# The tail of a recurrent block one step ahead, its hyperbolic tangent at the end of the block itself

## The chip, the cores and the metric

The kernel runs on one core of one Trainium2 chip. The metric is the device time of one execution, in microseconds; runs are compared by their medians.

## The reference

One layer with a prompt of 2048 tokens and 8 x 8 sample tokens (2112 columns in all) and a width of 1024. From the normalised input `u`, a projection `z = u @ w_in` feeds three branches: a recurrent one (RG-LRU), a dilated attention, and merge gates. The change touches the recurrent branch alone:

```python
xa, new_conv = causal_conv(xa, conv_buf, conv_w, conv_b)       # 4 taps
# rg_lru, in 8 blocks of 128 channels:
gate_a = einsum(x_block, w_a) + b_a ;  gate_x = einsum(x_block, w_x) + b_x
r = sigmoid(gate_a) ;  i = sigmoid(gate_x)
log_a = -8 * r * softplus(-lam)
a = exp(log_a)
u = sqrt(-expm1(2 * log_a)) * (i * x)
h_t = a_t * h_(t-1) + u_t                                      # along the tokens
ya = (hs * silu(ga)) @ w_lru_proj
```

## The kernel before

The order of the instructions is written out by hand: each engine takes its own in the order of the program, and waits only for semaphores. The stages run one after the other: normalising and transposing the input, the attention of the prompt, its gate, **the recurrent branch** (lines 815 to 975), the merge gates with the sample attention spread over them (`gm_block`, from line 991), and the output projections.

In the recurrent branch the loop over `b` does one block of 128 channels at a time. The tokens lie along the free dimension in five chunks `CH` of 512, 512, 384, 384 and 320 columns. A block has two halves of five steps; call them A0 to A4 and B0 to B4.

In A0 to A4, `zT` (24 matmuls, L760) projects one chunk for `xa`, and `evac` copies it (ScalarE, L861) into `xpad`. In between stand the convolutions of the chunks 0 and 1 (`conv`: one ScalarE instruction, L868, then three on VectorE, L870), the first `gates_a`, and the splits of weights into a high and a low half (`w_split`, `split`: a cast on ScalarE, L93, and a subtraction on VectorE, L94).

In B0 to B4, `zT` projects a chunk for the gate `ga`; ScalarE and VectorE make its silu in `sgl` (L964, L965); `gates_b` runs the six gate matmuls of the chunk (L888) on `xh`, the split copy of the convolved chunk that `gates_a` made (cast L879, subtraction L880), and turns them into `rr` and `ii` by sigmoids; then follow `gates_a` of the next chunk and, in B0 to B2, `conv` of the chunks 2 to 4. `xh` has one buffer, the z tiles of `zT` four (two tags of two).

What is left of a block, its tail, is done during the next block. `tail_1` makes `tt` = tanh from `rr` (five instructions, one for each chunk), `tail_2` the exponentials on ScalarE with a square on GpSimd and a product on VectorE, `tail_r` the square roots, and `tail_3` for each chunk a product (L914), the scan (L922), a product with `sgl` on GpSimd (L923) and a store to `Y1` (L924, on SP). Before, tail_1, tail_2 and tail_r stand at A0, A1 and A2, and the five pieces of tail_3 at A2, A3, A4, B0 and B1, each ahead of the convolution that writes the same chunk of `xc`. The tail of block 7 stands in the first `gm_block`. There `states` (its step 4) transposes the last states on TensorE into `hp` (L982).

DMAs are issued on SP in the order of the program: cache copies (`copy`, 480 KB each, one a step), weights (`w_raw`, one buffer), and the stores to `Y1`.

Of the kernel before, what the change touches and what calls it, by code (L numbers as in the profile page):

```python
# [42 lines left out]
def program(tc, I, O, C, upto=99, debug=False):  # L43
# [44 lines left out]
    def ztile(*tags):  # L88
        zi[0] += 1
        return ps.tile([128, 512], F32, name="zt", tag=tags[zi[0] % len(tags)])  # L90

    def split(h, l, src, eng):
        ACT.copy(h, src)  # L93
        eng.tensor_sub(l, src, h.bitcast(F32))  # L94
# [11 lines left out]
    def copy(n=1):  # L106
        for _ in range(n):
            if copies:
                i = dma(*copies.pop())
                if not G.manual:  # L110
                    tc.keep_in_program_order(i)
# [566 lines left out]
    def w_raw(src, nk=8):  # L678
        wr = wzp.tile([128, nk, 128], F32, name="wzr", tag="wzr")
        dma(wr, src)  # L680
        return wr

    def w_split(wr, eng, nk=8):
        w = wzp.tile([128, 2, nk, 128], F32R, name="wz", tag="wz", bufs=2)
        split(w[:, 0], w[:, 1], wr, eng)
        return w

    def wcols(c0):
        return win[:, c0:c0 + 128].rearrange("(k p) c -> p k c", p=128)
# [67 lines left out]
    def zT(z, w, c0, n):  # L757
        for i in range(24):
            k, p = divmod(i, 3)
            PE.matmul(z[:, 0:n], w[:, (0, 1, 0)[p], k, :], (RH, RH, RL)[p][:, k, c0:c0 + n], start=(i == 0), stop=(i == 23))  # L760
# [68 lines left out]
    def par_prep():  # L829
        prt = ps.tile([128, 8, 42], F32, name="prt", tag="tr")  # L830
        for n in range(8):
            PE.transpose(prt[:, n, :], rows[:, n * 128:(n + 1) * 128], ident[0:42, 0:42])
        DVE.tensor_copy(par, prt)
        DVE.tensor_scalar(e_, lam, -1.0, None, ALU.mult)
        DVE.tensor_tensor(e_, e_, lam, ALU.min)
        ACT.activation(e_, e_, AF.Exp)
        DVE.tensor_scalar(y_, e_, 2.0, None, ALU.add)
        DVE.reciprocal(y_, y_)
        DVE.tensor_mul(y_, y_, e_)
        DVE.tensor_mul(q_, y_, y_)  # L840
        DVE.tensor_scalar(c8, q_, 2.0 / 19, 2.0 / 17, ALU.mult, ALU.add)
        for i in (15, 13, 11, 9, 7, 5, 3, 1):
            DVE.tensor_mul(c8, c8, q_)
            DVE.tensor_scalar(c8, c8, 2.0 / i, None, ALU.add)
        DVE.tensor_mul(c8, c8, y_)
        DVE.tensor_scalar(e_, lam, -1.0, 0.0, ALU.mult, ALU.max)
        DVE.tensor_add(c8, c8, e_)
        DVE.tensor_scalar(n8, c8, 8.0, None, ALU.mult)
        DVE.tensor_scalar(c8, c8, -8.0, None, ALU.mult)
# [9 lines left out]
    def evac(c0, n, z):  # L859
        npr = min(n, SEQ - c0)  # L860
        ACT.copy(xpad[:, 3 + c0:3 + c0 + npr], z[:, 0:npr])  # L861
        if npr < n:
            ACT.copy(xsp[:, :, 3:11], z[:, npr:n].rearrange("p (s t) -> p s t", t=8))
# [13 lines left out]
    def gates_a(c0, n):  # L877
        xh = lp.tile([128, 2, 512], F32R, name="xh", tag="xh")
        ACT.copy(xh[:, 0, 0:n], xc[:, c0:c0 + n])  # L879
        DVE.tensor_sub(xh[:, 1, 0:n], xc[:, c0:c0 + n], xh[:, 0, 0:n].bitcast(F32))  # L880
        return xh
# [13 lines left out]
    def tail_1(b):  # L895
        for c0, n in CH:
            ACT.activation(tt[:, c0:c0 + n], rr[:, c0:c0 + n], AF.Tanh, scale=n8[:, b:b + 1])

    def tail_2(b):
        for c0, n in CH:  # L900
            s = slice(c0, c0 + n)
            ACT.activation(rr[:, s], rr[:, s], AF.Exp, scale=c8[:, b:b + 1])
            a2 = lp.tile([128, 512], F32, name="a2", tag="ii", bufs=2)
            POOL.tensor_mul(a2[:, 0:n], rr[:, s], rr[:, s])
            DVE.scalar_tensor_tensor(tt[:, s], a2[:, 0:n], 1.0, tt[:, s], ALU.add, ALU.mult)

    def tail_r(b):
        for c0, n in CH:
            ACT.activation(tt[:, c0:c0 + n], tt[:, c0:c0 + n], AF.Sqrt)

    def tail_3(b, i0=0, i1=5):
        for c0, n in CH[i0:i1]:
            s = slice(c0, c0 + n)
            DVE.tensor_mul(xc[:, s], xc[:, s], tt[:, s])  # L914
            if c0 + n == NT:
                a0 = rr[:, SEQ:NT:8]
                hh = lp.tile([128, 8], F32, name="hh", tag="hh")
                DVE.tensor_mul(hh, a0, par[:, b, 34:42])
                DVE.tensor_add(xc[:, SEQ:NT:8], xc[:, SEQ:NT:8], hh)
                DVE.memset(a0, 0.0)  # L920
            init = 0.0 if c0 == 0 else tt[:, c0 - 1:c0]
            DVE.tensor_tensor_scan(tt[:, s], rr[:, s], xc[:, s], init, ALU.mult, ALU.add)  # L922
            POOL.tensor_mul(sgl[:, s], sgl[:, s], tt[:, s])  # L923
            dma(Y1[b][:, s], sgl[:, s])  # L924
        if i1 < 5:
            return
        POOL.tensor_copy(par[:, b, 4:5], tt[:, SEQ - 1:SEQ])
        POOL.tensor_copy(par[:, b, 34:42], tt[:, SEQ + 7:NT:8])

    for b in range(8):  # L930
        for ci, (c0, n) in enumerate(CH):
            z = early.pop(ci, None) if b == 0 else None
            if z is None:
                z = ztile("z", "S")
                zT(z, wx, c0, n)
            evac(c0, n, z)
            copy()
            if ci == 0:
                gr = lp.tile([128, 2, 128], F32, name="gr", tag="gr")
                dma(gr[:, 0], I["lru_w_a"][0, b])  # L940
                dma(gr[:, 1], I["lru_w_x"][0, b])
                wga = w_split(wgr, DVE)
                wxr = w_raw(wcols((b + 1) * 128 if b < 7 else C_GM))
            if b == 0 and ci == 2:
                par_prep()
            if b and ci < 3:
                (tail_1, tail_2, tail_r)[ci](b - 1)
            if b and ci > 1:
                tail_3(b - 1, ci - 2, ci - 1)
            if ci == 2:  # L950
                POOL.tensor_copy(xsp[:, :, 0:3], par[:, b, 10:34].rearrange("p (s j) -> p s j", j=3))
                gw_ = lp.tile([128, 2, 2, 128], F32R, name="gw_", tag="gw_")
                split(gw_[:, 0], gw_[:, 1], gr, DVE)
                conv(b, *CH[0])
            if ci == 3:
                xh = gates_a(*CH[0])
                conv(b, *CH[1])
        for ci, (c0, n) in enumerate(CH):
            z = ztile("z", "S")
            zT(z, wga, c0, n)  # L960
            if ci == 0:
                wx = w_split(wxr, DVE)
                wgr = w_raw(wcols(1024 + (b + 1) * 128 if b < 7 else C_GM + 128))
            ACT.activation(sgl[:, c0:c0 + n], z[:, 0:n], AF.Sigmoid)  # L964
            DVE.tensor_mul(sgl[:, c0:c0 + n], z[:, 0:n], sgl[:, c0:c0 + n])  # L965
            gates_b(b, c0, n, xh, gw_)
            if ci < 4:
                xh = gates_a(*CH[ci + 1])
            if b and ci < 2:
                tail_3(b - 1, ci + 3, ci + 4)  # L970
            if ci < 3:
                conv(b, *CH[ci + 2])
            copy()
        POOL.tensor_copy(par[:, b, 0:3], xpad[:, SEQ:SEQ + 3])
        POOL.tensor_copy(par[:, b, 10:34].rearrange("p (s j) -> p s j", j=3), xsp[:, :, 8:11])

# [14 lines left out]
    def gm_block(f, w, hooks, gtile):  # L991
        for ci, (c0, n) in enumerate(CH):
            z = ztile("z", "S")
            zT(z, w, c0, n)
            for h in hooks.get(ci, ()):
                h()
            gt = gtile()
            ACT.activation(gt[:, 0:n], z[:, 0:n], AF.Sigmoid, bias=par[:, f % 8, 8 + f // 8:9 + f // 8])  # L998
            dma(Gsc[f][:, c0:c0 + n], gt[:, 0:n])
            copy()  # L1000
            if plan and f:
                for fn in plan.pop(0):
                    fn()

    plan = []
    wm = {0: wx}

    def nextw(f):
        if f + 1 < 16:
            wm[f + 1] = w_split(G.wr, DVE)  # L1010

    def nextr(f):
        if f + 2 < 16:
            G.wr = w_raw(wcols(C_GM + (f + 2) * 128))

    G.wr = wgr
    gm_block(0, wm[0], {0: (lambda: nextw(0), lambda: nextr(0), lambda: tail_1(7), lambda: tail_2(7)), 1: (lambda: tail_r(7), lambda: tail_3(7),), 4: (states,)},
             lambda: lp.tile([128, 512], F32, name="gt0", tag="ii", bufs=2))
    lr.close()
    gts = ExitStack()  # L1020
# [571 lines left out]
```

## Time and profile before

| | |
|---|---|
| median of 3 runs | 2575.45 us (2571.48 to 2576.32) |
| the profiled execution | 2570.03 us, span 2568.3 us |
| TensorE busy | 2501.8 us (97%) |
| VectorE, ScalarE, GpSimd busy | 1541.6, 1082.9, 561.5 us |
| mean granted TensorE clock | 0.992 |

The span is the time from the first to the last instruction of the profiled execution. An engine's busy time leaves out its waits; matmuls overlap, so a busy TensorE is not one at its peak. "Released by" names the instruction whose semaphore ended a wait.

### The profile page before, as it was taken

The numbers are of one execution on the slowest core, as the hardware profiler recorded it, in microseconds if no ns is written. First come the engines' busy times: TensorE is split into PE (matmuls) and PEld (weight loads), VectorE is DVE, ScalarE is ACT, GpSimd is POOL, SyncE is SP. The second block draws the span as 40 slices with busy tenths as digits, with TensorE's granted clock in tenths as the row PEclk, the third lists the DMA queues.
The fourth block names the chain that finished last, engine by engine and source line by source line (L and its number), as shares of the span: only waits on it lengthen the run. The fifth ranks groups of instructions, "written<-read, shape, count | busy, mean of one in ns | idle before, by whom it ended". The sixth has DMA issues, their size and how long they took to land. (4 is left out here: it accounts for less than half of the span.)

```text
span 2568.3 us, 44715 instructions
## 1 busy us (share of the span) xinstructions
PE 2501.8 (97%) x15196; PEld 2341.9 (91%) x15196; DVE 1541.6 (60%) x4805; ACT 1082.9 (42%) x3327; POOL 561.5 (22%) x897
## 2 busy tenths in 40 slices
PE   8999999999999999999999999999888999999999
PEld 7999999999999999999988888888878899998988
DVE  6744686777786776647665667737765723432322
ACT  5534453443553443444455655535466511211110
POOL 4423322221221221213233334320001012200000
PEclk9999999999999999999999999999999999999999
DMA  5443564555453433337633333345555479633332
GB/s 146 114 132 101 144 178 142 160 158 152 144 166 100 122 115 111 89 98 235 214 112 131 130 112 123 130 161 176 182 171 184 150 213 339 197 112 119 115 121 66
DMA packets 311288, 376.73 MB, mean 147 GB/s; under 512 B 54914, under 2 KB 254926, under 8 KB 308220
## 3 DMA queue, kind: packets, MB, share of 16 engines
q1 hardware_dynamic: 297028, 356.31, 45.2%
q0 software_dynamic: 14032, 17.57, 2.5%
q8 instruction: 120, 1.97, 0.3%
q14 instruction: 108, 0.88, 0.1%
HBM read 293.55 MB, written 168.31 MB: 180 GB/s over the span
## 5 line engine op out<-in xcount | busy, mean ns | idle before, releaser
L336 PE MATMUL z<-w,RH 128*128 128x384 f32 (+1 forms) x3088 | 889.1, 349 | 5.3 <-POOL w L317 2.4
L760 PE MATMUL zt<-RH,wz 128*128 128x384 f32 (+2 forms) x2560 | 701.4, 357 | 10.3 <-ACT gt L998 9.3
L336 PEld LDWEIGHTS z<-w,RH 128*128 128x128 f32 (+1 forms) x3088 | 553.3, 188 | 15.2 <-POOL w L317 6.3
L336 PE MATMUL z<-w,RL 128*128 128x384 f32 x1544 | 520.4, 337 | 0.1
L760 PEld LDWEIGHTS zt<-RH,wz 128*128 128x128 f32 x2560 | 467.5, 190 | 56.1 <-ACT gt L998 10.9
L760 PE MATMUL zt<-RL,wz 128*128 128x384 f32 (+2 forms) x1280 | 455.5, 356 | 0.0
L336 PEld LDWEIGHTS z<-w,RL 128*128 128x128 f32 x1544 | 291.4, 189 | 0.7 <-DVE RL L94 0.5
L178 DVE CUSTOM_DVE_ANT_0 kjk<-kt,qs 128x128 bf16<-128x128 f32 x768 | 228.4, 297 | 64.8 <-DMA qs<-QS 25.2
L760 PEld LDWEIGHTS zt<-RL,wz 128*128 128x128 f32 x1280 | 243.3, 190 | 22.0
L408 ACT ACTIVATE P<-P,o 128x128 f32<-128x128 f32 (+1 forms) x192 | 88.9, 463 | 309.0 <-DVE o L407 309.0
L345 ACT ACTIVATE jk<-z 128x128 bf16<-128x128 f32 (+1 forms) x408 | 113.2, 277 | 236.9 <-PE trc L376 173.6
L94 DVE TENSOR_TENSOR KQ<-trc,KQ 128x256 fp32r<-128x256 f32 x192 | 81.4, 424 | 209.1 <-ACT KQ L93 209.0
L347 POOL TENSOR_SCALAR ss<-ss 128x2 f32<-128x2 f32 (+1 forms) x204 | 44.3, 217 | 714.9 <-ACT jk L345 675.4
L1470 PEld LDWEIGHTS zt<-y1t,w_wlo 128*128 128x128 f32 x1536 | 190.3, 191 | 0.6
L1470 PE MATMUL zt<-y1t,w_wlo 128*128 128x256 f32 (+1 forms) x1536 | 190.6, 286 | 0.0
L1502 PE MATMUL zt<-w_wo,mt 128*128 128x512 f32 x672 | 162.0, 395 | 0.0
L1502 PEld LDWEIGHTS zt<-w_wo,mt 128*128 128x128 f32 x672 | 126.0, 188 | 30.7
L348 POOL TENSOR_TENSOR rs<-ss,neghalf 128x2 f32<-128x2 f32 (+1 forms) x204 | 142.5, 699 | 17.0
L1155 ACT ACTIVATE v<-v,P 128x128 f32<-128x128 f32 x256 | 81.1, 391 | 76.9 <-DMA v<-in_cache_kv_w 58.5
L434 DVE TENSOR_REDUCE o<-op 128x128 f32<-128x256 f32 x192 | 80.5, 419 | 44.8 <-PE op L429 44.7
L93 ACT CAST mt<-g 128x256 fp32r<-128x256 f32 x72 | 27.2, 388 | 187.3 <-DVE g L1473 172.1
L1504 DVE TENSOR_TENSOR xr<-zt,xr 128x512 f32<-128x512 f32 (+1 forms) x34 | 23.5, 692 | 137.3 <-PE zt L1502 132.6
(292 smaller groups left out, 4260.1 us busy)
## 6 DMA issues: line engine op xcount, KB each, us to landing
out_kv_s<-in_cache_kv_w SPq DMA_DIRECT2D x176, 480.0 KB
xt<-in_x_prompt SPq DMA_DIRECT2D x48, 512.0 KB
wr<-in_w_in SPq DMA_DIRECT2D x96, 192.0 KB
kt<-in_cache_kv_w SPq DMA_DIRECT2D x128, 128.0 KB
wzr<-in_w_in SPq DMA_DIRECT2D x32, 512.0 KB
v<-in_cache_kv_w SPq DMA_DIRECT2D x128, 128.0 KB
Osc<-o SPq DMA_DIRECT2D x192, 65.0 KB
ot<-Osc SPq DMA_DIRECT2D x32, 390.0 KB
```

Source lines behind the costliest of these rows:

```text
L94: eng.tensor_sub(l, src, h.bitcast(F32))
L178: DVE.tensor_tensor_reduce(jk, kts[q.tile][:, c], qts[t][:, c], 1.0, 0.0, ALU.mult, ALU.add, q.SC[:, o:o + 1])
L336: PE.matmul(u.z[0:m, :], (RH, RL, RH)[p][:, k, u.cols], Wt[(u.g, u.h), k][:, (0, 0, 1)[p], :], start=(i == 0), stop=(i == 23))
L345: ACT.activation(jk[0:m, :], z[0:m, i * 128:(i + 1) * 128], AF.Square, accum_out=u.ss[0:m, i:i + 1])
L347: POOL.tensor_scalar(u.ss[0:m, :], u.ss[0:m, :], 1.0 / HD, EPS, ALU.mult, ALU.add)
L348: POOL.tensor_tensor(u.rs[0:m, :], u.ss[0:m, :], neghalf[0:m, :], ALU.pow)
L408: ACT.activation(u.P[:, 0:n], u.P[:, 0:n], AF.Exp, bias=u.o[:, 128:129], scale=-1.0, accum_out=u.o[:, 129:130])
L434: DVE.tensor_reduce(u.o[:, 0:128], u.op.rearrange("p a b -> p b a"), AX.X, ALU.add)
L760: PE.matmul(z[:, 0:n], w[:, (0, 1, 0)[p], k, :], (RH, RH, RL)[p][:, k, c0:c0 + n], start=(i == 0), stop=(i == 23))
L1155: ACT.activation(v2s[n][:, h], v2s[n][:, h], AF.Copy, scale=P2[:, h, n:n + 1])
L1470: PE.matmul(z[:, 0:n], wl[k][:, (0, 1, 0)[p], f, :], y1s[c * 8 + k][:, (0, 0, 1)[p], 0:n], start=(i == 0), stop=(i == 23))
L1502: PE.matmul(z[0:m, :], ms_[k][:, (0, 0, 384)[p] + o:(0, 0, 384)[p] + o + m], wo[k][:, (0, 1, 0)[p], e * 4:(e + 1) * 4, :].rearrange("p k c ...
```

## The change

The tanh of a block (`tail_1`) moves from A0 of the next block to the end of the block itself. Exponentials (`tail_2`) and square roots (`tail_r`) move from A1 and A2 to A0 and A1. The pieces 0 to 4 of `tail_3` move from A2, A3, A4, B0, B1 to A1, A2, A3, A4, B0. In the first `gm_block`, `tail_1(7)` goes, as block 7 has done it, and `tail_3(7)` is cut in two calls, for the chunks 0 and 1 in step 1 and 2 to 4 in step 2.

```diff
-            if b and ci < 3:
-                (tail_1, tail_2, tail_r)[ci](b - 1)
-            if b and ci > 1:
-                tail_3(b - 1, ci - 2, ci - 1)
+            if b and ci < 2:
+                (tail_2, tail_r)[ci](b - 1)
+            if b and ci > 0:
+                tail_3(b - 1, ci - 1, ci)
...
-            if b and ci < 2:
-                tail_3(b - 1, ci + 3, ci + 4)
+            if b and ci == 0:
+                tail_3(b - 1, 4, 5)
             if ci < 3:
                 conv(b, *CH[ci + 2])
             copy()
+        tail_1(b)
         POOL.tensor_copy(par[:, b, 0:3], xpad[:, SEQ:SEQ + 3])
...
-    gm_block(0, wm[0], {0: (lambda: nextw(0), lambda: nextr(0), lambda: tail_1(7), lambda: tail_2(7)), 1: (lambda: tail_r(7), lambda: tail_3(7),), 4: (states,)},
+    gm_block(0, wm[0], {0: (lambda: nextw(0), lambda: nextr(0), lambda: tail_2(7)), 1: (lambda: tail_r(7), lambda: tail_3(7, 0, 2)), 2: (lambda: tail_3(7, 2, 5),), 4: (states,)},
```

## Rows read from the trace of the kernel before

**Rows 1.** The page's busy us, share of the span and instructions of each engine.

```profile
PE 2501.8 (97%) x15196; PEld 2341.9 (91%) x15196; DVE 1541.6 (60%) x4805; ACT 1082.9 (42%) x3327; POOL 561.5 (22%) x897
```

**Rows 2.** Stretches: length, busy us of each engine, granted clock, DMA share, GB/s.

```profile
1302.70:1678.40 375.70, 366.81 (x1893) 327.33 (x1892) 251.59 (x344) 222.04 (x379) 143.58 (x140) 1.00 0.39 126
1678.40:2100.00 421.60, 392.55 (x2041) 353.99 (x2040) 250.29 (x899) 209.01 (x542) 31.16 (x46) 0.96 0.54 170
...
1700.00:1706.70 6.70, 5.29 (x13) 4.17 (x14) 1.42 (x3) 0.58 (x1) 1.58 (x4) 0.50 0.78 257
```

**Rows 3.** Waits of TensorE, whole span: us in total, times, longest.

```profile
PE OT L1220 <- DVE vt L94: 12.3, 1, 12.3
...
PE zga L888 <- ACT xh L879: 8.5, 7, 1.2
PE hp L982 <- POOL par L928: 5.4, 1, 5.4
```

**Rows 4.** Gate matmuls of blocks 0, 1, 7: duration, first and last start.

```profile
L888 PE MATMUL zga<-xh,gw__17474 x30: 308/338/398, 1273.8 to 1296.8; 128*128 128x512 f32 x12, 128*128 128x384 f32 x12, 128*128 128x320 f32 x6
L888 PE MATMUL zga<-xh,gw__17902 x30: 307/350/499, 1325.3 to 1350.4; 128*128 128x512 f32 x12, 128*128 128x384 f32 x12, 128*128 128x320 f32 x6
...
L888 PE MATMUL zga<-xh,gw__20602 x30: 307/352/503, 1647.1 to 1672.1; 128*128 128x512 f32 x12, 128*128 128x384 f32 x12, 128*128 128x320 f32 x6
```

**Rows 5.** Timeline of TensorE, block 2, second half: start, us, idle before.

```profile
1378.93 1.57 PE L888 MATMUL zga<-xh,gw__18352 128*128 128x512 f32 x6
...
1385.93 1.80 PE L888 MATMUL zga<-xh,gw__18352 128*128 128x512 f32 x6
1387.57 0.51 PE L760 MATMUL zt<-RH,wz 128*128 128x384 f32 x2
...
1391.56 0.34 PE L760 MATMUL zt<-RL,wz 128*128 128x384 f32 x1
1393.12 1.56 PE L888 MATMUL zga<-xh,gw__18352 128*128 128x384 f32 x6 [1.22 <-ACT xh L879]
```

**Rows 6.** Timeline of ScalarE, block 2 and the end of block 7.

```profile
1357.71 2.80 ACT L897 ACTIVATE tt<-rr,cc 128x512 f32<-128x512 f32 x5
...
1362.38 1.28 ACT L902 ACT_TABLE_LOAD   x1
1363.68 2.81 ACT L902 ACTIVATE rr<-rr,cc 128x512 f32<-128x512 f32 x5
...
1371.23 0.47 ACT L909 ACTIVATE tt<-tt 128x320 f32<-128x320 f32 x1 [0.58 <-DVE tt L905]
...
1380.82 1.28 ACT L964 ACT_TABLE_LOAD   x1
...
1410.04 0.59 ACT L861 COPY xpad<-zt 128x512 f32<-128x512 f32 x1 [4.92 <-PE zt L760]
...
1678.02 2.81 ACT L902 ACTIVATE rr<-rr,cc 128x512 f32<-128x512 f32 x5
```

**Rows 7.** Timeline of VectorE, block 2.

```profile
1371.12 0.68 DVE L914 TENSOR_TENSOR xc<-xc,tt 128x512 f32<-128x512 f32 x1
...
1386.41 1.64 DVE L914 TENSOR_TENSOR xc<-xc,tt 128x384 f32<-128x384 f32 x1
...
1389.03 3.45 DVE L870 SCALAR_TENSOR_TENSOR xc<-xpad,par,xc 128x384 f32<-128x384 f32 x3
...
1393.58 0.48 DVE L914 TENSOR_TENSOR xc<-xc,tt 128x320 f32<-128x320 f32 x1
...
1395.21 2.40 DVE L870 SCALAR_TENSOR_TENSOR xc<-xpad,par,xc 128x384 f32<-128x384 f32 x3
```

**Rows 8.** VectorE groups by shape, blocks 1 to 7: busy us, mean ns.

```profile
L914 DVE TENSOR_TENSOR xc<-xc,tt 128x384 f32<-128x384 f32 x14 | 15.3, 1095 | 0.0
...
L922 DVE TENSOR_TENSOR_SCAN tt<-rr,tt,xc 128x384 f32<-128x384 f32 x14 | 14.3, 1018 | 0.5
```

**Rows 9.** Waits of SP's DMA queue, blocks 1 to 7: us, times, longest.

```profile
SPq L924 <- POOL sgl L923: 223.2, 35, 13.7
```

## The prediction

> **What bounds the kernel now.** I read the busy shares first, then the stretches, then who waits for whom, then the timeline of one block on each engine. TensorE is busy 97% of the span and no other engine over 60% [rows 1]; so only time in which TensorE waits, or runs at half clock, can be won, and work saved elsewhere counts only through such a wait. The recurrent branch (the loop over b) fills 1302.7 to 1678.4 us for blocks 1 to 7; there TensorE is busy 366.8 of 375.7 us at a granted clock of 1.00, the DMA engines 0.39 [rows 2]. The waits name what is missing: 8.5 us in 7 waits, one for each of the blocks 1 to 7, in which the gate matmuls of L888 want `xh` from the cast of L879 [rows 3]. The timeline of block 2 shows the place, the third chunk: the last projection matmul before it starts at 1391.56 and the gates at 1393.12 [rows 5].
>
> The wait costs more than its 1.2 us, because the first and last passes around it are stretched too. Block 0 has no tail of an earlier block to do, and is the measure: its 30 gate matmuls, with the four projections between them, run from 1273.8 to 1296.8, 23.0 us; in the blocks 1 to 7 the same takes 25.0 to 25.3, seven times, 176.0 us together [rows 4]. So 176.0 - 7 x 23.0 = 15.0 us stand above what TensorE needs.
>
> Why is `xh` late? VectorE arrives late. It starts the last products of the tail (L914 of the first chunk) at 1371.12 [rows 7], since these wait for the square roots, and those for exponentials that start at 1363.68 [rows 6]. At 1386.41 it still has pieces four and five of the tail ahead, one of which (product 1.64, then a scan) stands before the convolution of the third chunk, 1389.03 + 3.45 = 1392.48 [rows 7]; the gates follow 0.64 later, at 1393.12 [rows 5].
>
> **The change part by part.**
>
> *The five tanh (tail_1) at the block's end.* Same count, same 2.80 us for the five [rows 6]. They fall into ScalarE's idle time before the next block's first evacuation, 4.92 us [rows 6]; they read `rr`, which ScalarE itself has just written. Cost nothing; without that cover they would delay that evacuation by 2.8 us, which four z tiles absorb. Tables: in both orders the table changes before the exponentials, before the square roots and before the next sigmoid; no load appears in front of the tanh now (its start 1357.71 follows the cast directly) and none should after. If one did, 1.28 us would still fit in the 4.92.
>
> *Exponentials and square roots one step earlier.* The exponentials take the place of the tanh: 1357.71 + 1.28 load + 0.02 = 1359.01 instead of 1363.68 [rows 6], 4.67 earlier. They end at 1361.82, where the second evacuation is due (the load now at 1362.38 follows it directly), so that one is late by some 0.1 us. The five square roots come before the third evacuation. The last of them ran at 1371.23 for 0.47, waiting for VectorE [rows 6]; 4.67 earlier it ends at 1367.0. The third evacuation, which stood at about 1366.4 between exponentials and load, is late by 0.6. Who waits for that? TensorE reuses that z tile four projections later, at the one that starts with the second gate projection after 1378.93 + some 1.4 = 1380.3 [rows 5]: margin 13 us, cost nothing.
>
> *The pieces of tail_3.* They move by one step: pieces 0 to 4 stand at A1, A2, A3, A4, B0 (A and B the two halves of a block) instead of A2, A3, A4, B0, B1. VectorE does the same instructions. Up to the point that is 1386.41 now it has one piece more to do: a product of 384 columns, mean 1.10, and a scan, 1.02 [rows 8], so it gets there at 1386.41 - 4.67 + 2.12 = 1383.9. ScalarE gives about the same: the gate half's first sigmoid can't run before its matmuls end near 1379.0 [rows 5], then load 1.28 [rows 6] and four pieces of 0.6, cast ready near 1382.9, its subtraction on VectorE 1383.7. Then piece 4, now from 1393.58 to 1395.21, 1.63; then the third convolution, 3.45 as now or 2.40 as the fourth [rows 7]: done at 1383.9 + 1.63 + 2.40 to 3.45 = 1387.9 to 1389.0, and 0.64 for the cast 1388.6 to 1389.6. TensorE would ask for it at about 1391.7 (last matmul 1391.56 [rows 5]), less 0.3 that the second gates, now 1.64 from 1385.93 to 1387.57, would win. Margin 1.8 to 2.8 us; the wait is gone. The second gates get their low half 2 us earlier as well. After that VectorE has one piece less (piece 4 no longer lies between the convolutions of chunks 3 and 4), and no later wait shows: the fourth and fifth gates would have about 2 us more. Gain between nothing and 15.0; I take all, as the margin is over the largest duration seen.
>
> Here the Trainium skill speaks against it (ScalarE: Activation LUTs, "What ACT_TABLE_LOAD costs"): a switch costs about 2.66 us, a load and then a drain. The trace differs: the load at 1362.38 is followed by an exponential at 1363.68, 1.30 later [rows 6]. By the page's figure two switches would put the tail 2.7 us later, over the margin by about 0.9 in the worst case, and the gain would be 15.0 - 7 x 0.9 = 8.7.
>
> *Transfers.* Each piece issues one store (L924) and SP waits for its product on GpSimd: 223 us in 35 such waits [rows 9]. Behind these stand cache copies and the load of `wgr`; all go out earlier, none is added. The same bytes in 15 us less raise a DMA share of 0.39 to 0.41 [rows 2]. Nothing.
>
> *After block 7.* Tanh and the weight split only change places on ScalarE; the exponentials start at 1678.02 as now [rows 6], measured from TensorE's end of block 7. The split of tail_3 into 0 to 2 and 2 to 5 puts nothing between its parts on VectorE or GpSimd; on SP one gate store and one copy move ahead of three stores. So the wait of 5.4 us of the transposes `hp` for the last state [rows 3], and the half clock behind it (0.50 in 1700 to 1706.7 [rows 2]), stay. Bounds: nothing to 8.0 gained (5.4 and half of the 5.3 us in which TensorE then ran at half speed); I take nothing, since the chain to it starts at the same place.
>
> *Sum.* 15.0 us off the profiled execution's 2570.0 (its span 2568.3) gives 2555.0. The median of the runs is 2575.45, 5.4 above that execution, so I forecast 2575.45 - 15.0 = 2560.5. A difference of 0.2%, about 5 us, is what a measurement of this kernel can tell from none.
>
> **The rivals.**
>
> *Half is left (faster, less).* The tail's GpSimd products collide with VectorE elsewhere: a product of 384 columns took 1.64 at 1386.41 against a mean of 1.10, the convolution 3.45 against 2.40 [rows 7, 8]. If pieces 1 to 4 were all slowed by 0.35 and the convolutions of chunks 0 and 1 by 1 each, VectorE would be 3.4 us later, 0.6 to 1.6 beyond the margin: 4 to 11 us lost over seven blocks, in the middle 7.5 left, 2568. Against: GpSimd's products come sooner and further apart. Chance 0.14.
>
> *No change.* The time won is given back behind the branch. In 1678.4 to 2100 TensorE waits 12.3 us for `vt` [rows 3], in a stretch where the cache decides (DMA share 0.54 [rows 2]); were that stretch held by transfers that don't start sooner, up to 15 would be lost: 2570 to 2575. Against: its loads go into buffers that open only after the branch, so they shift with it. Chance 0.09.
>
> *Slower.* At A1 the ScalarE queue stands still for VectorE's last product while evacuations, casts and the gate weights' split wait behind the square roots. That decides when the time from the first exponential to the last square root grows from 8.0 us (1363.68 to 1371.70 [rows 6]) by more than the 13 us of the z tile. Were it 16 longer, TensorE would lose 3 us in each block, 21 in all, and the gain of 15 would be gone: 2575.45 + 6 = 2581. For it speaks only that GpSimd and VectorE pass two buffers to and fro there; the chain's instructions are unchanged. Chance 0.07.
>
> **How the numbers follow.** All of the 15 has a chance of 0.70 (own range 2556 to 2565, the spread of the runs, 2571 to 2576, on either side). Half 0.14, none 0.09, slower 0.07. Time 2560.5. Range: down to 2553, 7 of the 8.0 at the end of the branch; up to 2572, which takes in half and the better part of none. Faster by over 0.2%: 0.70 + 0.14 = 0.84; within 0.2%: 0.09; slower: 0.07.
>
> **What would show it.** The gate matmuls of each block 1 to 7 spanning about 23 us; no wait of L888 for L879; tanh inside an idle stretch of ScalarE at the block's end; three table loads a block; the branch (1302.7 to 1678.4) at about 361 us; the wait for `hp` still 5 us. I am wrong if the wait of L888 stays or moves to another chunk, if TensorE waits at an evacuation (L861), or if the branch is shorter and the stretch behind it longer.

## The result, and the profile after

| | before | after |
|---|---|---|
| median | 2573.22 us (2570.18 to 2576.32, 6 runs) | 2557.86 us (2554.25 to 2565.94, 6 runs) |
| ratio, 95% interval | | 0.9944 (0.9927 to 0.9961) |
| profiled execution, span | 2570.03, 2568.3 us | 2556.18, 2554.4 us |
| first gate matmul of block 0 to last of block 7 | 1273.8 to 1672.1, 398.3 us | 1275.0 to 1659.0, 384.0 us |
| from there to the end of the span | 896.2 us | 895.4 us |

The medians lie 15.4 us apart, the spans 13.9. A second comparison, beside the later experiments, gave 0.9939 (0.9926 to 0.9951). The three parts of the span add up: the stages before the branch, which the diff does not touch, took 1.2 us longer in this execution, the branch 14.3 less, everything behind it 0.8 less.

In the rows PE is TensorE, PEld its loading of weights, DVE VectorE, ACT ScalarE, POOL GpSimd, and SP the engine whose queue issues the DMAs. The busy shares of the page after, and the stretches that answer to [rows 1, 2] (length, busy us of each engine, granted clock, DMA share, GB/s):

```profile
PE 2493.1 (98%) x15196; PEld 2340.1 (92%) x15196; DVE 1546.4 (61%) x4805; ACT 1081.5 (42%) x3327; POOL 557.9 (22%) x897
```

```profile
1303.90:1664.50 360.60, 360.60 (x1890) 328.52 (x1890) 257.19 (x344) 218.13 (x373) 140.84 (x140) 1.00 0.40 130
1664.50:2084.00 419.50, 388.09 (x2025) 349.21 (x2024) 250.56 (x900) 209.57 (x543) 31.35 (x46) 0.96 0.54 171
...
1686.70:1693.40 6.70, 5.11 (x15) 4.09 (x16) 2.83 (x4) 1.46 (x2) 1.58 (x4) 0.58 0.78 255
```

In the branch TensorE is now busy in all of 360.6 us. What stands behind it is as long as it was. The waits of TensorE (us in total, times, longest) show the same: no line for the gate matmuls, the waits for `vt` and for the last state within 0.1 of [rows 3]. The z tiles wait for the merge gates (`gt`) for 12.0 us, 9.3 before.

```profile
PE OT L1221 <- DVE vt L94: 12.2, 1, 12.2
PE zt L760 <- ACT gt L999: 12.0, 5, 5.4
...
PE hp L983 <- POOL par L928: 5.3, 1, 5.3
```

The gate matmuls of the blocks 0, 1 and 7, as in [rows 4]: each block now takes 23.0 to 23.1 us, like block 0.

```profile
L888 PE MATMUL zga<-xh,gw__17474 x30: 307/338/399, 1275.0 to 1298.1; 128*128 128x512 f32 x12, 128*128 128x384 f32 x12, 128*128 128x320 f32 x6
...
L888 PE MATMUL zga<-xh,gw__17906 x30: 308/338/398, 1326.6 to 1349.6; 128*128 128x512 f32 x12, 128*128 128x384 f32 x12, 128*128 128x320 f32 x6
...
L888 PE MATMUL zga<-xh,gw__20606 x30: 308/339/399, 1636.0 to 1659.0; 128*128 128x512 f32 x12, 128*128 128x384 f32 x12, 128*128 128x320 f32 x6
```

Block 2 on TensorE, ScalarE, VectorE and GpSimd (start, us, what; idle before and who ended it). This execution's block 2 stands 0.80 us earlier than that of [rows 5 to 7] (gates of the first chunk at 1378.13 and 1378.93); add 0.80 to compare.

```profile
1385.12 1.56 PE L888 MATMUL zga<-xh,gw__18356 128*128 128x512 f32 x6
...
1390.69 1.21 PE L888 MATMUL zga<-xh,gw__18356 128*128 128x384 f32 x6
```

```profile
1350.46 2.79 ACT L897 ACTIVATE tt<-rr,cc 128x512 f32<-128x512 f32 x5
1355.49 0.59 ACT L861 COPY xpad<-zt 128x512 f32<-128x512 f32 x1 [2.23 <-PE zt L760]
...
1357.04 1.28 ACT L902 ACT_TABLE_LOAD   x1
1358.33 2.80 ACT L902 ACTIVATE rr<-rr,cc 128x512 f32<-128x512 f32 x5
1361.04 0.56 ACT L861 COPY xpad<-zt 128x512 f32<-128x512 f32 x1
...
1365.88 0.47 ACT L909 ACTIVATE tt<-tt 128x320 f32<-128x320 f32 x1 [0.58 <-DVE tt L905]
1366.26 0.46 ACT L861 COPY xpad<-zt 128x384 f32<-128x384 f32 x1
...
1388.43 0.51 ACT L879 CAST xh<-xc 128x384 fp32r<-128x384 f32 x1 [1.02 <-DVE xc L870]
```

```profile
1365.77 0.68 DVE L914 TENSOR_TENSOR xc<-xc,tt 128x512 f32<-128x512 f32 x1
...
1383.22 1.57 DVE L914 TENSOR_TENSOR xc<-xc,tt 128x320 f32<-128x320 f32 x1
...
1385.94 2.40 DVE L870 SCALAR_TENSOR_TENSOR xc<-xpad,par,xc 128x384 f32<-128x384 f32 x3
...
1388.97 0.94 DVE L880 TENSOR_TENSOR xh<-xc,xh 128x384 fp32r<-128x384 f32 x1
```

```profile
1382.71 1.74 POOL L893 TENSOR_TENSOR xc<-xc,ii 128x512 f32<-128x512 f32 x1
```

The tanh run in ScalarE's idle time and leave 2.23 us of it; the exponentials start at 1358.33; the third convolution ends on VectorE at 1388.34, the cast of `xh` at 1388.94, its subtraction at 1389.91, and the gates start at 1390.69 without a wait.

### The profile page after: what moved, and what is told of

Its sections match the earlier page's. It is cut to its first block, busy times and chain, and to the rows that moved or that the text cites. A ratio compares the mean times of both kernels' runs of the same rounds, so it can differ in the third digit from the quotient of the medians.

```text
span 2554.4 us, 44714 instructions
## 1 busy us (share of the span) xinstructions
PE 2493.1 (98%) x15196; PEld 2340.1 (92%) x15196; DVE 1546.4 (61%) x4805; ACT 1081.5 (42%) x3327; POOL 557.9 (22%) x897
## 4 chain that ended last, share of the span: by engine, by line
PE 83%; DMA 6%; DVE 5%; ACT 3%; issue 1%; SPq 1%; POOL 1%; DVEq 0%; ACTq 0%; POOLq 0%
PE z L336 28%; PE zt L760 22%; PE zt L1471 7%; PE zt L1503 7%; PE zt L534 3%; PE zt L1415 3%; PE zga L888 2%; DMA v<-in_cache_kv_w 2%; PE trx L247 1%; PE op L428 1%; PE S L406 1%; DVE kjk L178 1%; PE tre L416 1%; DMA xt<-in_x_prompt 1%; PE trc L376 1%
```

## The experiments

Four kernels take the change apart, two load VectorE in the changed kernel, and the last ones try the places that the change left. Each ratio is to the kernel before, measured beside it.

**The tanh alone.** The kernel before with one part of the change; `tail_1(7)` leaves the first `gm_block` as well.

```diff
-            if b and ci < 3:
-                (tail_1, tail_2, tail_r)[ci](b - 1)
+            if b and 0 < ci < 3:
+                (tail_2, tail_r)[ci - 1](b - 1)
...
+        tail_1(b)
         POOL.tensor_copy(par[:, b, 0:3], xpad[:, SEQ:SEQ + 3])
...
```

> The kernel before with one edit: the five tanh stand at the end of their own block; exponentials, square roots and the pieces of tail_3 stay at their old steps. Theory (the gain comes from the tail's start, that is from the exponentials): the exponentials still stand behind the second evacuation, at 1363.7 on block 2's clock, so VectorE is as late as before: gate matmuls of a block 25.1 us, seven waits of L888 for L879, time of before within 2 us. Rival A (the tanh themselves held ScalarE up where it mattered): part of the 14 us comes, 5 us or more.

Measured: 2571.24 us, ratio 1.0001 (0.9992 to 1.0011). Block 1's gate matmuls and the wait, the same as before:

```profile
L888 PE MATMUL zga<-xh,gw__17902 x30: 307/350/499, 1326.0 to 1351.1; 128*128 128x512 f32 x12, 128*128 128x384 f32 x12, 128*128 128x320 f32 x6
```

```profile
PE zga L888 <- ACT xh L879: 8.5, 7, 1.2
```

Rival A falls: taking 2.8 us of tanh out of the start of a block is worth nothing while the exponentials wait for the second evacuation.

**All but the tanh.** The changed kernel with the tanh back in front of the exponentials (block 7's in the first `gm_block`); the exponentials, the roots and the pieces keep their new steps.

```diff
+            if b and ci == 0:
+                tail_1(b - 1)
             if b and ci < 2:
                 (tail_2, tail_r)[ci](b - 1)
...
-        tail_1(b)
         POOL.tensor_copy(par[:, b, 0:3], xpad[:, SEQ:SEQ + 3])
...
```

> The changed kernel with the tanh back at the start of the next block, ahead of the exponentials; all steps stand ahead as in the change. Theory: the exponentials start at 1357.7 + 2.8 + 1.3 = 1361.8, 1.9 earlier than before and 2.8 later than in the change. The changed kernel has 1.75 us to spare for the high half of xh of the third chunk and 1.1 for the low half, so about 0.2 to 1.2 us of wait come back in each block: gate matmuls 23.3 to 24.3 us, 6 to 14 of the 14.5 us kept, middle 10. Rival B (only the written order of the pieces counts): all 14.5 kept. Rival A (only the tanh): nothing kept.

Measured: 2569.47 us, ratio 0.9992 (0.9983 to 1.0002); gate matmuls 24.7 to 24.8 us in each block. So hardly 2 us are kept, not 10, and the interval of the ratio reaches beyond 1. Block 2 on TensorE shows where my estimate was short: the first gates wait for the low half, 0.22 us, and the third for both halves, 0.27 and 0.35 us.

```profile
1378.12 1.20 PE L888 MATMUL zga<-xh,gw__18356 128*128 128x512 f32 x4 [0.22 <-DVE xh L880]
...
1390.81 0.61 PE L888 MATMUL zga<-xh,gw__18356 128*128 128x384 f32 x2 [0.27 <-ACT xh L879]
1391.77 0.97 PE L888 MATMUL zga<-xh,gw__18356 128*128 128x384 f32 x4 [0.35 <-DVE xh L880]
```

The waits that are shown make 0.84 us; the block lost 1.7. A gate pass, from its first matmul to the next projection, took 1.39, 1.40, 1.05, 1.05 and 0.88 us in the five chunks of the changed kernel, and 1.89, 1.55, 1.76, 1.05 and 0.87 here: the first three lost time, each more than its idle time (the second shows none). I had priced a late `xh` at its idle time. Rival B falls too: the written order of the pieces is not the gain.

**The early start alone.** The changed kernel with the pieces of tail_3 back at their old steps.

```diff
-            if b and ci > 0:
-                tail_3(b - 1, ci - 1, ci)
+            if b and ci > 1:
+                tail_3(b - 1, ci - 2, ci - 1)
...
-            if b and ci == 0:
-                tail_3(b - 1, 4, 5)
+            if b and ci < 2:
+                tail_3(b - 1, ci + 3, ci + 4)
```

> The changed kernel with the five pieces of tail_3 back at their old steps (A2, A3, A4, B0, B1); tanh, exponentials and square roots stay ahead. Theory: VectorE is held by ScalarE's sigmoids at the first gates until about 1383.3, then piece 3 (2.6) and the third convolution (2.4 to 3.5) end at 1388.3 to 1389.4 as in the change; piece 4 then lies in front of the fourth convolution, whose gates have 2 us to spare: no wait, all 14.5 us kept, gate matmuls 23.0 to 23.2. Rival B (the order of the pieces counts): the wait of the third gates comes back, half or more of the 14.5 us lost.

Measured: 2555.35 us, ratio 0.9943 (0.9929 to 0.9958): the whole gain, with gate matmuls of 23.0 to 23.1 us in every block. Block 1:

```profile
L888 PE MATMUL zga<-xh,gw__17902 x30: 308/338/398, 1328.4 to 1351.5; 128*128 128x512 f32 x12, 128*128 128x384 f32 x12, 128*128 128x320 f32 x6
```

These three together say what does it: neither the tanh's place (0) nor the new steps without it (2 us of 14), but that the exponentials start right behind the first evacuation. That takes both the tanh out of the way and tail_2 one step ahead; tail_r goes with them in both kernels that gain. Block 2 shows it as a dose. The exponentials start 15.3 us ahead of the first gates in the kernel before and with the tanh alone moved, 17.1 in the second of these kernels and 19.8 in the changed kernel and the third; the gate matmuls take 25.1 to 25.3, 24.7 and 23.0 to 23.1 us.

**The third convolution first.** The kernel before, where the convolution of the third chunk passes piece 3.

```diff
+            if ci == 0:
+                conv(b, *CH[2])
             if b and ci < 2:
                 tail_3(b - 1, ci + 3, ci + 4)
-            if ci < 3:
+            if 0 < ci < 3:
                 conv(b, *CH[ci + 2])
```

> The kernel before with one edit: at B0 the convolution of the third chunk stands in front of piece 3 of the tail and not behind it; tanh, exponentials, square roots and pieces keep their steps. Theory (VectorE reaches the third convolution too late): the convolution starts at 1386.4 in place of 1389.0, the high half of xh is in time, its subtraction, now behind piece 3, comes at 1392.3 to 1394 against 1392.1: gate matmuls of a block 23.2 to 24.7 us, 3 to 13 us faster than before, middle 8. If the wait came from anything but VectorE's order at this place (a transfer, the z tiles, ScalarE's queue), nothing changes.

Measured: 2569.74 us, ratio 0.9994 (0.9985 to 1.0003); gate matmuls 24.9 us in most blocks. Of the 3 to 13 us that I expected hardly 2 came, and the interval reaches beyond 1: the wait went to the next chunk. TensorE in block 2, third and fourth chunk:

```profile
1391.71 0.51 PE L888 MATMUL zga<-xh,gw__18352 128*128 128x384 f32 x2
...
1392.41 0.97 PE L888 MATMUL zga<-xh,gw__18352 128*128 128x384 f32 x4 [0.20 <-DVE xh L880]
...
1398.34 1.56 PE L888 MATMUL zga<-xh,gw__18352 128*128 128x384 f32 x6 [0.79 <-ACT xh L879]
```

The third gates start in time with their high half and wait for the low one; the fourth now wait 0.79 us, because the pieces 3 and 4 still have to be done before the fourth convolution. So it is not the one place that is late but VectorE's whole queue through the second half: letting one instruction pass another moves the debt, starting the tail sooner pays it.

**A load on VectorE.** The changed kernel with products that compute nothing that is used, in the second half's first step; three in one kernel, twelve in the other.

```diff
+    junk = lp.tile([128, 160], F32, name="junk")
...
+    POOL.memset(junk, 1.0)
...
                 tail_3(b - 1, 4, 5)
+                for _ in range(3):                 # 12 in the second kernel
+                    DVE.tensor_mul(junk, junk, junk)
```

> The changed kernel with three idle products of 160 columns on VectorE (about 0.75 us together) in each block, between piece 4 of the tail and the third convolution. They compute nothing that is used. Theory: the high half of xh of the third chunk has 1.75 us to spare in the changed kernel, the low half 1.1; 0.75 goes into that: no wait, gate matmuls 23.1 us, time of the changed kernel within 2 us. Rival (the changed kernel stands just at the edge, or VectorE's work itself sets the time): 0.75 x 7 = 5 us slower.

> The same with twelve such products, about 3 us in each block. Theory: 3 - 1.1 = 1.9 us too late for the low half, 1.2 for the high half; the gate passes stretch by 1.6 to 2.2 us in each block (23.1 to about 25), 11 to 15 us slower than the changed kernel, so the time of before. Rival (VectorE has slack over the whole block, busy 36 of 52 us, and takes it up): the time of the changed kernel.

Measured: 2560.51 us, 0.9962 (0.9949 to 0.9975), gate matmuls 23.8 us; and 2600.55 us, 1.0115 (1.0101 to 1.0129), 28.5 us in block 1 and 29.2 to 29.5 in the others. Beside the changed kernel's 2555.62 us that is 4.9 us more, where I expected none, and 44.9, where I expected 11 to 15. Both cost more than I expected, first because the load was twice what I meant. The three products took 1.58 us, the twelve 5.80 (VectorE; the group of the first kernel; TensorE's third gates; then the second kernel):

```profile
1385.06 1.58 DVE L974 TENSOR_TENSOR junk<-junk 128x160 f32<-128x160 f32 x3
1386.57 2.95 DVE L872 SCALAR_TENSOR_TENSOR xc<-xpad,par,xc 128x384 f32<-128x384 f32 x3
```

```profile
L974 DVE TENSOR_TENSOR junk<-junk x21: 298/326/892, 1332.8 to 1647.7; 128x160 f32<-128x160 f32 x21
```

```profile
1390.17 1.56 PE L890 MATMUL zga<-xh,gw__18361 128*128 128x384 f32 x6 [0.33 <-ACT xh L881]
```

```profile
1390.64 5.80 DVE L974 TENSOR_TENSOR junk<-junk 128x160 f32<-128x160 f32 x12
```

```profile
1398.93 2.29 PE L890 MATMUL zga<-xh,gw__18370 128*128 128x384 f32 x6 [3.50 <-ACT xh L881]
```

With the sizes that came out, the margin of 1.75 us for the high half holds. Measured from the first gates of the block, the third convolution ends after 10.21 us in the changed kernel (1378.13 to 1388.34), after 12.27 with three products (1377.25 to 1389.52): 2.06 - 1.75 = 0.31, and TensorE waits 0.33. With twelve it ends after 15.46 (1382.82 to 1398.28): 5.25 - 1.75 = 3.50, and it waits 3.50. The 4.9 us are by chance what the rival forecast: were there no margin, the 2.06 us would have cost 14 in seven blocks. The price of such a wait is again above its idle time: with three products the projection before the gates and the gates themselves lost 0.48 and 0.36 against the changed kernel. With twelve, the granted clock falls as well, as told at the end. VectorE is busy for some 70% of the branch, and has no slack that would take up even 2 us at this place.

**The end of the branch.** The changed kernel with the tail of block 7 in another order.

```diff
-            POOL.tensor_mul(sgl[:, s], sgl[:, s], tt[:, s])
-            dma(Y1[b][:, s], sgl[:, s])
+            if b < 7:
+                POOL.tensor_mul(sgl[:, s], sgl[:, s], tt[:, s])
+                dma(Y1[b][:, s], sgl[:, s])
...
-        POOL.tensor_copy(par[:, b, 4:5], tt[:, SEQ - 1:SEQ])
-        POOL.tensor_copy(par[:, b, 34:42], tt[:, SEQ + 7:NT:8])
+        eng = POOL if b < 7 else DVE
+        eng.tensor_copy(par[:, b, 4:5], tt[:, SEQ - 1:SEQ])
+        eng.tensor_copy(par[:, b, 34:42], tt[:, SEQ + 7:NT:8])
+        for c0, n in CH if b == 7 else ():
+            s = slice(c0, c0 + n)
+            DVE.tensor_mul(sgl[:, s], sgl[:, s], tt[:, s])
+            dma(Y1[b][:, s], sgl[:, s])
...
-    gm_block(0, wm[0], {0: (..., lambda: tail_2(7)), 1: (lambda: tail_r(7), lambda: tail_3(7, 0, 2)), 2: (lambda: tail_3(7, 2, 5),), 4: (states,)},
+    gm_block(0, wm[0], {0: (..., lambda: tail_2(7), lambda: tail_r(7)), 1: (lambda: tail_3(7, 0, 5),), 4: (states,)},
```

> The changed kernel with another end of the branch: the square roots of block 7 ahead of the first merge-gate sigmoid (two table loads less in that chain), and for block 7 the products with sgl and the copies of the last state on VectorE behind all five scans, with the stores behind them. Theory: the last state is ready some 7 us sooner, before TensorE asks for it; the wait of 5.3 us of the transposes and the half clock behind it (2.6 us) go: 8 us faster than the changed kernel, about 2550, 0.991 of before. Rival: the stretch behind, where TensorE waits 12 us for the cache values, takes it up: that wait grows by as much and the time stays at 0.9945.

> The changed kernel again, for comparison in the same chip and hour: 0.9945 of before, within 0.001.

Measured: 2553.87 us, 0.9928 (0.9915 to 0.9941), beside 2555.62 us, 0.9939 (0.9926 to 0.9951) for the changed kernel. The medians differ by 1.8 us, not 8, and the intervals overlap: in time this is inconclusive. In the trace the wait for the last state is gone and the granted clock stays at 1.00 from 1664 to 1710, but from the last gate matmul to the first matmul of the next stage it still takes 415.5 us (1664.0 to 2079.5). The changed kernel beside it has 419.4 (1658.3 to 2077.7), and the five traces in which this stretch has the same code spread from 416.8 to 419.6: of the 8 us between 1 and 4 are left. The wait for `vt` did not take them up; it is 12.0 us in both. The first place where TensorE then waits, and what ScalarE waits for in 1690 to 1760:

```profile
1718.79 1.22 PE L760 MATMUL zt<-RH,wz 128*128 128x512 f32 x2 [2.44 <-ACT gt L1005]
```

```profile
ACT gt L1005 <- DMA Gsc<-gt: 39.1, 7, 18.0
```

ScalarE cannot write the next merge gate before the store of an earlier one has landed, and these stores stand on SP among the cache loads of the sample attention.

**The merge gates' stores on another queue.** The kernel with the other end and the changed kernel, with the stores of the merge gates 1 to 14 issued by GpSimd.

```diff
-            dma(Gsc[f][:, c0:c0 + n], gt[:, 0:n])
+            (POOL.dma_start if 0 < f < 15 else dma)(Gsc[f][:, c0:c0 + n], gt[:, 0:n])
```

> The kernel with the other end of the branch, and the stores of the merge gates (f 1 to 14) issued on GpSimd's queue in place of SP's. Theory (behind the branch TensorE waits for z tiles, since ScalarE waits for gt, whose stores stand behind cache loads on SP): the waits of L760 for the gate sigmoid, 10 to 12 us, shrink to under 4, and the 8 us won at the branch's end are kept: 10 us or more under the changed kernel, 0.990 of before. Rival: the chain of the cache values (wait of 12 us for vt) grows by what the others lose, and the time stays at 0.993.

> The changed kernel with the stores of the merge gates on GpSimd's queue alone. Theory: the waits of L760 for the gate sigmoid (10 to 12 us) shrink to under 4, 4 to 8 us under the changed kernel, 0.9915 of before. Rival: the wait for vt takes it up, 0.994.

Measured: with the other end 2543.98 us, 0.9887 (0.9871 to 0.9904); alone 2547.26 us, 0.9898 (0.9881 to 0.9916). Both beat the changed kernel. The last gate matmul and the first one of the next stage, and the waits, with both edits:

```profile
L888 PE MATMUL zga<-xh,gw__20606 x30: 307/338/398, 1637.9 to 1660.9; 128*128 128x512 f32 x12, 128*128 128x384 f32 x12, 128*128 128x320 f32 x6
```

```profile
L1421 PE MATMUL zt<-ytl,w_wa x768: 280/285/361, 2070.1 to 2167.0; 128*128 128x264 f32 x192
```

```profile
PE OT L1227 <- DVE vt L94: 10.5, 1, 10.5
PE zt L760 <- ACT gt L1005: 6.3, 2, 4.8
PE trp L1106 <- ACT SA L1094: 4.9, 1, 4.9
```

The stretch is 409.2 us long, 10 less than in the changed kernel; with the queue alone 414.3 (1656.9 to 2071.2). The wait for z tiles fell from 10.4 us (12.0 in the execution shown above) to 6.3, and to 6.6 with the queue alone, not under 4. The wait for `vt` did not grow (10.5 and 12.0 us, beside 12.0), so its rival falls; with both edits TensorE waits 4.9 us for `SA`, 0.6 with the other end alone. In time the queue alone is worth 8 us by the medians (2555.62 to 2547.26); of the 6.1 us between the two profiled executions 1.5 stand ahead of the branch, where the code is the same.

The gain is shown, its path is not. Waits of ScalarE and of SP's queue from 1660 to 2080, in the changed kernel and then with both edits:

```profile
ACT v L1156 <- DMA v<-in_cache_kv_w: 70.2, 31, 8.4
ACT gt L999 <- DMA Gsc<-gt: 36.5, 9, 13.4
...
SPq L1000 <- ACT gt L999: 94.4, 34, 8.1
```

```profile
ACT v L1162 <- DMA v<-in_cache_kv_w: 39.9, 16, 8.8
ACT gt L1005 <- DMA Gsc<-gt: 37.3, 11, 9.2
...
SPq L1006 <- ACT gt L1005: 28.0, 8, 9.7
```

ScalarE waits for the stores as long as before. What fell is the time in which SP's queue stood still at such a store until ScalarE had made the gate, and ScalarE's wait for cache values, some of whose loads stand behind it on SP. With the queue alone all three fell (59.8, 24.9 and 24.8 us). So the stores may have held up the loads as much as the loads the stores; no run parts the two.

## Why the prediction was right

The forecast was 15.0 us less; the medians show 15.4, the branch in the traces 14.3. The time itself, 2557.86 us, lies 2.6 under the 2560.5 of the forecast, mostly since the median of the kernel before is 2573.22 over six runs and was 2575.45 over the three that were known. Step by step:

*What is to be won.* The excess over block 0, seven times, was the right measure, although the wait itself is listed with only 8.5 us. It came out at 14.6 by the gate matmuls (176.0 before, 161.4 after).

*The tanh.* Hidden, as forecast: 2.23 of the 4.92 us [rows 6] are left. The tanh-only kernel shows that its move is also worth nothing by itself.

*The start of the tail.* Forecast 1359.01, 1361.8 and 1367.0 for the first exponential, the second evacuation and the end of the last root; measured 1359.13, 1361.84 and 1367.15 (0.80 added). The third evacuation is late by 0.67, as forecast 0.6, and nobody waits for it. From the first exponential to the last root it still takes 8.0 us, so the rival "slower" falls. The one table load between a cast and an exponential took 1.29 us from its start to the exponential's (1357.04 to 1358.33). The Trainium skill (ScalarE: Activation LUTs, "What ACT_TABLE_LOAD costs") gives 2.66 us for a switch; neither that nor the 8.7 us reckoned from it shows in the trace after.

*VectorE's queue.* Forecast for piece 4: 1383.9; measured 1384.0. For the end of the third convolution 1387.9 to 1389.0; measured 1389.1, just past the late end, for a reason that I had priced wrongly: piece 4 took 2.72 us and not 1.63. Its product of 320 columns, 0.48 us in [rows 7], took 1.57. It began at 1383.22, in the middle of GpSimd's product (1382.71 to 1384.45), and ended 0.3 us behind that. The Trainium skill says of this (SBUF — State Buffer, "Who interferes with whom") that a VectorE instruction with two inputs in SBUF and a GpSimd instruction that reads SBUF exclude each other, and that the later one waits for the whole of the earlier; these rows agree. That is the mechanism of the rival "half is left", against which I had said that GpSimd's products come further apart; it cost 1.1 us here, inside the margin.

*The margin.* Forecast 1.8 to 2.8 us; measured 1.75 for the high half (1388.94 to 1390.69), and the kernels with a load on VectorE agree with that number. I had not priced the low half, which is the nearer: subtraction done at 1389.91 and asked for some 0.3 us behind 1390.69, 1.1 us to spare. The gain was safe, but by half of what I said; with the tanh back in front, 2.7 us later, nearly all of it is gone.

*The order of the pieces.* I had costed the steps of tail_3 as part of what makes the change work. The kernel with the old steps has the whole gain without them.

*Behind the branch.* The wait for the last state stayed (5.4 and 5.3 us), as did the half clock (0.50 and 0.58 in the same 6.7 us). The rival "no change" did not come about: the time won inside the blocks was kept, since the stretch behind them moved with TensorE. From the last gate matmul to the first one of the next stage it is 419.4 us before and 418.8 after. Time that is won at the end of the branch is another matter, as the kernel with the other end shows: 1 to 4 of 8 us stay in that stretch, some 5 with the stores on the other queue (414.3 to 409.2, one trace of each). What takes the rest is not shown.

## What to carry to other kernels

Where one engine sets the time, compare equal pieces of work with and without the suspected delay, instead of adding up its listed waits: block 0 gave the gain to within 5%, the waits little more than half. A consumer that is late again and again may be late from its first instruction of the round: ask what lets that one start, before changing the order of the last ones; here moving the start by 4.55 us was worth 14 us, and passing one instruction in front of another moved the wait to the next chunk. And a step that is moved into idle time paid here only through what then moved up behind it.

## What the runs showed of the hardware

Short waits cost TensorE more than they show. With three products on VectorE, 0.33 us of idle time in front of the third gates cost 0.84 us in that place. The waits listed for the weight loads come nearer. In the kernel before, those for `xh` in the blocks 1 to 7 make 16.5 us, where 14.6 were won and the list of the matmuls has 8.5:

```profile
PEld zga L888 <- ACT xh L879: 10.8, 7, 1.5
PEld zga L888 <- DVE xh L880: 5.7, 15, 0.6
```

A longer wait also costs clock. Behind the 3.50 us in which TensorE waited with twelve products on VectorE, the granted clock was about half for the next 5.7 us and full again after that (1.2 and 2.4 GHz); behind the waits of 1.2 us in the kernel before it stayed at 1.00 [rows 2]. Stretches of the kernel with twelve products:

```profile
1398.90:1404.60 5.70, 5.67 (x18) 5.58 (x19) 5.08 (x9) 3.35 (x7) 1.01 (x1) 0.53 0.65 197
1404.60:1410.00 5.40, 5.40 (x35) 5.40 (x35) 2.61 (x6) 2.00 (x4) 1.02 (x1) 1.00 0.02 3
```

A VectorE product of 160 columns took 0.30 us at best and up to 0.89: in block 2 the second of three, from 1385.40 to 1386.29, ran beside a GpSimd product that stood from 1385.23 to 1386.11, so that a load meant as 0.75 us became 1.58.
